# Feed-forward operands of TensorE begin at other places in a 256-byte stretch of SBUF

## The chip, the core and the metric

The kernel runs on one core of a Trainium2 chip. The time is device time in microseconds (us), from one execution to the next of the same program; the change is judged by the median of several runs. TensorE multiplies, VectorE (DVE) and ScalarE (ACT) do the elementwise work, and a DMA queue on SyncE (SP) brings the weights from HBM. SBUF has 128 partitions; where a tile "begins" below means its byte address in a partition, and only its rest after division by 256 is named.

## What is computed

Two layers, each of which holds two half-step feed-forward blocks; they are what the change touches:

```python
def swiglu(h, w1, w3, w2):
    return (jax.nn.silu(h @ w1) * (h @ w3)) @ w2
...
for l in range(DEPTH):                                   # DEPTH = 2
    x = x + 0.5 * swiglu(rms_norm(x, ffn1_norm_g[l]), ffn1_w1[l], ffn1_w3[l], ffn1_w2[l])
    ...                                                  # mixer: one projection, three branches, w_out
    x = x + cross_attention(rms_norm(x, xattn_norm_g[l]), ...)
    x = x + 0.5 * swiglu(rms_norm(x, ffn2_norm_g[l]), ffn2_w1[l], ffn2_w3[l], ffn2_w2[l])
return rms_norm(x, final_norm_g)
```

There are 256 tokens, a width of 1024 and a feed-forward width of 2816, all in float32.

## The kernel before

**Products in two parts.** TensorE works in fp32r, which keeps fewer bits of a float32. So each factor is split into a high part (the value rounded to fp32r) and a low part (what is left), and a product a·b is made as hi·hi + hi·lo + lo·hi. Weights come from HBM as float32 into `w_raw`; `_split` (L108) lets ACT write the high part `w_hi` (L126) and DVE the low part `w_lo` (L127). The activations are kept in two parts side by side: `xn` (the normed input, 8 blocks of 128 features), `g` (the inner activation, 22 blocks), `mix`, `mem_n`, `o`.

**The feed-forward products.** `ffn` (L472) goes over two column blocks of w1 and w3 at a time with `gemm_w` (L365), and at its end over w2. Each step is `mm_w` (L259), two passes of TensorE, in which a block of 128x128 weights is stationary and the activations move past it:

- the hi pass: stationary `w_hi`, moving both parts of `xn` or `g`, 512 columns;
- the lo pass: stationary `w_lo`, moving the high part alone, 256 columns.

So a stretch of feed-forward work is hi, lo, hi, lo, and so on, each with new weights. I call one hi pass and one lo pass a pair. w1 and w3 take 352 pairs in each of four blocks, w2 takes 176 in each of the first three. The last w2 is computed the other way round (`final`, L519): there the weights move, 512 columns in every pass, and `g` is stationary.

**Where tiles begin.** The tiles for `w_hi` and `w_lo` have 64 elements more than the weights need, and the weights begin `at_` elements into them (L114 to L117, table `W_AT`, L39). `xn` and `g` lie in the same manner in tiles with room to spare (`placed`, L289, with `XN_AT`, L37, and `G_AT`, L41). In the built program the tiles themselves begin 128 (`w_hi`, `w_lo`), 64 (`xn`) and 160 (`g`) past a multiple of 256, in every buffer, and a step from one block to the next is a multiple of 512 bytes. With the offset (4 bytes an element) that gives, for the passes that stand in this document, the table below; "distance" is the beginning of the stationary operand less that of the moving one.

| passes | columns | moving begins | stationary begins | distance |
|---|---|---|---|---|
| feed-forward, hi | 512 | 96 | 192 | 96 |
| feed-forward, lo | 256 | 96 | 192 | 96 |
| last w2 (weights move) | 512 | 64 | 64 | 0 |
| mixer, weights move (`w_hi<-xn` groups) | 512 | 96 | 96 | 0 |
| w_out, o, q projections | 256 | 160, 160, 96 | 128, 128, 64 | -32 |
| memory keys / values | 256 / 512 | 64 / 64 | 32 / 64 | -32 / 0 |
| attention scores and values | 256 | 160 | 160 | 0 |

**What sets the order.** A scheduler fixes the order on each engine when the program is built; it doesn't look at addresses. Weights are loaded into two buffers and split into three, so ACT and DVE work ahead of TensorE.

Of the kernel before, what the change touches and what calls it, by code (L numbers as in the profile page):

```python
# [9 lines left out]
F32R = mybir.dt.float32r  # L10
# [5 lines left out]
P = 128  # L16
# [8 lines left out]
CW = 256  # L25
# [5 lines left out]
PART_BUFS = 3  # L31
# [2 lines left out]
QE_BUFS = 1  # L34
T3_BUFS = 8
PAD = {"xn": 16, "g": 128, "mix": 0}
XN_AT = {"ffn1": 8, "mix": 8, "xattn": 8, "ffn2": 8}  # L37

W_AT = {("w13", False): 16, ("w1", False): 16, ("w3", False): 16, ("w2", False): 16, ("w2", True): 48,  # L39
        ("in", True): 56, ("kv", False): 40, ("kv", True): 48, ("out", False): 0, ("o", False): 0, "other": 48}  # L40
G_AT = (48, 40)  # L41
MIX_AT = 0
X_LOADS = ((0, 1), (1, 1), (2, 2), (4, 2), (6, 2))
T4_BUFS = 6
# [17 lines left out]
class Weights:  # L62
# [45 lines left out]
    def _split(self):  # L108
        nc, i = self.nc, self.n_split
        self.n_split += 1  # L110
        u, unit, at, nk = self.steps[i]
        while self.n_load < len(self.pieces) and self.pieces[self.n_load][0] <= u:
            self._load()
        at_ = W_AT.get((unit.key, unit.beside), W_AT["other"])  # L114
        hi = self.pool.tile([P, 4 * CW + 64], F32R, name="w_hi", tag="w_hi", bufs=PART_BUFS)[:, at_:at_ + 4 * CW]
        lo = self.pool.tile([P, 4 * CW + 64], F32R, name="w_lo", tag="w_lo", bufs=PART_BUFS)[:, at_:at_ + 4 * CW]
        if unit.key == "w13":  # L117
            hi, lo = (t[:, 0:2 * nk * CW].rearrange("p (h k c) -> p h k c", h=2, k=nk) for t in (hi, lo))
            t = self._both(u, at).rearrange("p (h k c) -> p h k c", h=2, k=nk)
        elif unit.beside:  # L120
            hi, lo = (t.rearrange("p (h k c) -> p h k c", h=2, k=2)[:, :, 0:nk, :] for t in (hi, lo))
            t = self.raw[u].rearrange("p h (k c) -> p h k c", k=4)[:, :, at:at + nk, :]
        else:
            hi, lo = (t.rearrange("p (k c) -> p k c", k=4)[:, 0:nk, :] for t in (hi, lo))
            t = self.raw[u].rearrange("p h (k c) -> p h k c", k=4)[:, at, 0:nk, :]
        self.last = nc.scalar.copy(hi, t)  # L126
        nc.vector.tensor_tensor(out=lo, in0=t, in1=hi.bitcast(F32), op=ALU.subtract)  # L127
        self.parts[i] = (hi, lo)
# [88 lines left out]
def trunk(ctx: ExitStack, tc: tile.TileContext, a: dict, out: bass.AP, stop=None, dbg=None):  # L217
# [71 lines left out]
    def placed(pool, name, k, at, **kw):  # L289

        n = k * 2 * S
        return pool.tile([P, n + PAD[name]], F32R, name=name, bufs=1, **kw)[:, at:at + n].rearrange(
            "p (k u s) -> p k u s", k=k, u=2)
# [132 lines left out]
    class Norm:  # L426


        def __init__(self, l, name, mem=False):
            self.gains = col(l, name)  # L430
            if not mem:
                self.x = placed(keep, "xn", KD, XN_AT[name.split("_")[0]], tag="xn")
            self.ssq = small.tile([P, S], F32, name="ssq", tag="ssq", bufs=2)
# [38 lines left out]
    def ffn(l, f, nrm, nxt, last=False, setup=None):  # L472
        with tc.tile_pool(name="ffn", bufs=2) as fp:
            g = placed(fp, "g", KF, G_AT[last])
            if setup is not None:
# [814 lines left out]
```

## Time and profile before

| | |
|---|---|
| median of 3 runs | 1233.04 us (1232.77 to 1233.06) |
| the profiled execution | 1232.75 us |
| its span, first to last instruction | 1231.0 us |
| TensorE (PE) busy | 1220.6 us, 99% of the span |
| weight loads (PEld) | 1100.8 us, 89% |
| DVE busy | 935.7 us, 76% |
| ACT busy | 738.3 us, 60% |
| granted TensorE clock | 0.998 of full speed |

Matmuls overlap: the next one begins before the one ahead has come out of the array, so the length of a single record (some 390 ns for 512 columns) is more than the time from one start to the next (some 230 ns). Where I speak of the time per pass, it is from start to start over a long run of passes; where I speak of the length of a record, it is compared with the length of other records of the same shape only. The numbers of the trace are rounded to 0.01 us for starts and to 1 ns for mean lengths.

### The profile page before, as it was taken

The page shows a single profiled execution, that of the slowest core. Times are in us where ns is not written, and L with a number is a line of the kernel's source. Part 1 is how long each engine was busy: PE and PEld are TensorE (multiplying, and loading weights), DVE is VectorE, ACT ScalarE, POOL GpSimd, SP SyncE. Part 2 cuts the span into 40 slices and gives each one's busy share as a digit, 9 for nine tenths or more (in the row PEclk, how much of TensorE's full clock was granted, in tenths as well). Part 3 has the DMA queues.
Part 4 walks back from the last instruction along what each step waited for, and adds up shares of the span by engine and source line. Part 5 has one row for each costly group of instructions (what it writes and reads, how often), then busy time and mean ns, then how long its engine had stood idle before and what let it go on. Part 6 is the DMA issues. An engine that isn't in the chain of part 4 may idle for free.

```text
span 1231.0 us, 21670 instructions
## 1 busy us (share of the span) xinstructions
PE 1220.6 (99%) x8378; PEld 1100.8 (89%) x8378; DVE 935.7 (76%) x1649; ACT 738.3 (60%) x1309; POOL 30.5 (2%) x54
## 2 busy tenths in 40 slices
PE   9999999999999999999999999999999999999997
PEld 8888889988999988888888888899898999888886
DVE  6989866888777687786678886679787767778754
ACT  6766645556765665664466654465677646656643
POOL 1000000000100000000000000000000000000000
PEclk9999999999999999999999999999999999999999
DMA  7645555443344345455555455544434534555453
GB/s 253 251 182 190 173 190 200 146 163 138 137 173 171 125 184 200 177 205 188 189 216 204 177 200 188 188 171 155 155 138 146 196 137 155 192 185 200 177 188 120
DMA packets 62568, 219.32 MB, mean 178 GB/s; under 512 B 6912, under 2 KB 8192, under 8 KB 62208
## 3 DMA queue, kind: packets, MB, share of 16 engines
q1 hardware_dynamic: 60976, 213.35, 47.6%
q0 software_dynamic: 768, 3.86, 0.8%
q8 instruction: 66, 1.08, 0.3%
q10 hardware_dynamic: 720, 0.72, 0.2%
q14 instruction: 38, 0.31, 0.1%
HBM read 216.85 MB, written 1.05 MB: 177 GB/s over the span
## 4 chain that ended last, share of the span: by engine, by line
PE 95%; DVE 3%; ACT 1%; issue 1%; DMA 0%; POOLq 0%; POOL 0%; ACTq 0%; DVEq 0%
PE mm L243 87%; PE aux L243 2%; PE aux L833 1%; DVE w_lo L127 1%; DVE qe L814 0%; PE aux L831 0%; DMA xT<-in_x_t_dram 0%; PE mm L241 0%; ACT w_hi L126 0%; PE aux L241 0%; DVE xc L908 0%; PE aux L826 0%; PE aux L983 0%; PE aux L912 0%; PE aux L1104 0%
## 5 line engine op out<-in xcount | busy, mean ns | idle before, releaser
L127 DVE TENSOR_TENSOR w_lo<-w_raw,w_hi 128x1024 fp32r<-128x1024 f32 (+1 forms) x411 | 494.6, 1205 | 213.5 <-ACT w_hi L126 208.3
L126 ACT CAST w_hi<-w_raw 128x1024 fp32r<-128x1024 f32 (+1 forms) x411 | 425.1, 1035 | 360.5 <-PE mm L243 217.6
L243 PE MATMUL mm<-xn,w_hi 128*128 128x512 f32 (+1 forms) x2028 | 601.1, 359 | 1.6 <-ACT ssq L440 0.9
L243 PE MATMUL mm<-xn,w_lo 128*128 128x256 f32 x1728 | 476.9, 281 | 0.0
L243 PEld LDWEIGHTS mm<-xn,w_hi 128*128 128x128 f32 x2028 | 357.6, 188 | 57.2 <-ACT w_hi L126 1.1
L243 PEld LDWEIGHTS mm<-xn,w_lo 128*128 128x128 f32 x1728 | 324.7, 188 | 3.7
L243 PE MATMUL mm<-g,w_hi 128*128 128x512 f32 x528 | 180.8, 392 | 0.0
L243 PE MATMUL mm<-g,w_lo 128*128 128x256 f32 x528 | 141.9, 280 | 0.0
L243 PEld LDWEIGHTS mm<-g,w_hi 128*128 128x128 f32 x528 | 96.6, 188 | 19.0
L243 PEld LDWEIGHTS mm<-g,w_lo 128*128 128x128 f32 x528 | 99.4, 188 | 2.9
L243 PE MATMUL mm<-w_hi,xn 128*128 128x512 f32 (+1 forms) x318 | 89.1, 374 | 0.0
L493 ACT COPY f_p<-mm 128x256 f32<-128x256 f32 x176 | 63.8, 365 | 24.5 <-PE mm L243 23.6
L494 DVE TENSOR_TENSOR f_t<-mm,f_p 128x256 f32<-128x256 f32 x176 | 73.1, 418 | 2.5 <-ACT f_p L493 2.4
L243 PEld LDWEIGHTS mm<-w_hi,xn 128*128 128x128 f32 x318 | 57.2, 188 | 9.2
L498 DVE TENSOR_TENSOR f_t<-f_t,R 128x512 f32<-128x512 f32 x88 | 60.2, 688 | 1.6 <-ACT R L462 0.4
L243 PE MATMUL mm<-w_lo,xn 128*128 128x512 f32 (+1 forms) x160 | 56.6, 378 | 1.0 <-DVE w_lo L127 1.0
L243 PE MATMUL mm<-w_hi,g 128*128 128x512 f32 x176 | 51.9, 390 | 0.0
L243 PE MATMUL mm<-mem_n,w_hi 128*128 128x256 f32 x248 | 46.7, 284 | 0.0
L243 PE MATMUL mm<-o,w_hi 128*128 128x256 f32 x248 | 46.2, 281 | 0.0
L466 DVE SCALAR_TENSOR_TENSOR xT<-mm,xT 128x256 f32<-128x256 f32 x80 | 32.1, 420 | 17.3 <-PE mm L243 17.3
L243 PE MATMUL mm<-mix,w_hi 128*128 128x256 f32 x256 | 44.8, 279 | 0.0
L243 PE MATMUL mm<-w_hi,mem_n 128*128 128x512 f32 x128 | 39.5, 393 | 0.0
(253 smaller groups left out, 1476.6 us busy)
## 6 DMA issues: line engine op xcount, KB each, us to landing
w_raw<-in_weights_dram SPq DMA_DIRECT2D x395, 512.0 KB, 4.0
w_raw<-in_weights_dram SPq DMA_DIRECT2D x18, 256.0 KB, 3.6
m_t<-in_mem_t_dram POOLq DMA_DIRECT2D x2, 1024.0 KB, 6.4
xT<-in_x_t_dram SPq DMA_DIRECT2D x3, 256.0 KB, 6.4
cst<-in_c_cst_dram POOLq DMA_DIRECT2D x1, 696.0 KB, 4.4
out_dram<-yg SPq DMA_DIRECT2D x2, 320.0 KB, 2.5
gw<-in_gates_w_dram POOLq DMA_DIRECT2D x2, 256.0 KB, 6.8
fg<-in_final_norm_g_dram POOLq DMA_DIRECT2D x1, 512.0 KB, 5.8
```

Source lines behind the costliest of these rows:

```text
L126: self.last = nc.scalar.copy(hi, t)
L127: nc.vector.tensor_tensor(out=lo, in0=t, in1=hi.bitcast(F32), op=ALU.subtract)
L243: i = self.last = nc.tensor.matmul(acc, lhsT, rhs, start=begin, stop=stop, skip_group_check=True)
L466: nc.vector.scalar_tensor_tensor(out=xT[:, j, :], in0=h, scalar=scale, in1=xT[:, j, :], op0=ALU.mult, op1=ALU.add)
L493: nc.scalar.copy(p, banks[m][:, 1, :])
L494: nc.vector.tensor_tensor(out=t[m][:, u, :], in0=banks[m][:, 0, :], in1=p, op=ALU.add)
L498: nc.vector.tensor_tensor(out=t[m], in0=t[m], in1=nrm.R[:, None, :].to_broadcast([P, 2, S]), op=ALU.mult)
L833: nc.tensor.matmul(sb[bs, i, :], ke[:, 1 + i, cb], qe[:, 1 + i, cb], start=True, stop=True, skip_group_check=True)
```

## The change

The feed-forward parts get offsets of their own, the high and the low part each its own, and `xn` (in the four feed-forward blocks) and `g` move too. All other entries keep their value, now written as a pair.

```diff
-XN_AT = {"ffn1": 8, "mix": 8, "xattn": 8, "ffn2": 8}
+XN_AT = {"ffn1": 0, "mix": 8, "xattn": 8, "ffn2": 0}
-W_AT = {("w13", False): 16, ("w1", False): 16, ("w3", False): 16, ("w2", False): 16, ("w2", True): 48,
-        ("in", True): 56, ("kv", False): 40, ("kv", True): 48, ("out", False): 0, ("o", False): 0, "other": 48}
-G_AT = (48, 40)
+W_FF = (48, 40)
+W_AT = {("w13", False): W_FF, ("w1", False): W_FF, ("w3", False): W_FF, ("w2", False): W_FF, ("w2", True): (48, 48),
+        ("in", True): (56, 56), ("kv", False): (40, 40), ("kv", True): (48, 48), ("out", False): (0, 0),
+        ("o", False): (0, 0), "other": (48, 48)}
+G_AT = (40, 40)
...
-        hi = self.pool.tile([P, 4 * CW + 64], F32R, name="w_hi", tag="w_hi", bufs=PART_BUFS)[:, at_:at_ + 4 * CW]
-        lo = self.pool.tile([P, 4 * CW + 64], F32R, name="w_lo", tag="w_lo", bufs=PART_BUFS)[:, at_:at_ + 4 * CW]
+        hi = self.pool.tile([P, 4 * CW + 64], F32R, name="w_hi", tag="w_hi", bufs=PART_BUFS)[:, at_[0]:at_[0] + 4 * CW]
+        lo = self.pool.tile([P, 4 * CW + 64], F32R, name="w_lo", tag="w_lo", bufs=PART_BUFS)[:, at_[1]:at_[1] + 4 * CW]
```

The tiles stay where they were; only the beginnings inside them move. In the built program the instructions of every engine, their order and their waits are the same as before. The feed-forward rows of the table become:

| passes | columns | moving begins | stationary begins | distance |
|---|---|---|---|---|
| feed-forward, hi | 512 | 64 | 64 | 0 |
| feed-forward, lo | 256 | 64 | 32 | -32 |

All other rows stay as they were, the last w2 among them.

## Rows read from the trace of the kernel before

**Rows 1.** The page: busy time by engine, and the chain that ended last.

```profile
PE 1220.6 (99%) x8378; PEld 1100.8 (89%) x8378; DVE 935.7 (76%) x1649; ACT 738.3 (60%) x1309; POOL 30.5 (2%) x54
PE 95%; DVE 3%; ACT 1%; issue 1%; DMA 0%; POOLq 0%; POOL 0%; ACTq 0%; DVEq 0%
```

**Rows 2.** Waits of PE: total us, times, longest.

```profile
PE mm L243 <- DVE w_lo L127: 1.0, 2, 0.5
PE mm L243 <- ACT ssq L440: 0.9, 1, 0.9
```

**Rows 3.** Feed-forward stretches: length, busy us (count) by engine, clock, DMA.

```profile
core 0: us, PE busy (x) PEld busy (x) DVE busy (x) ACT busy (x) POOL busy (x), PEclk, DMA share, GB/s
432.73:555.74 123.01, 123.01 (x713) 108.30 (x712) 99.65 (x162) 73.94 (x134) 0.70 (x1) 1.00 0.51 189
555.74:616.82 61.08, 61.08 (x354) 53.77 (x353) 37.27 (x55) 29.58 (x41) 0.00 (x0) 1.00 0.54 190
```

**Rows 4.** PE groups by shape, whole span: count, busy us, mean ns, idle before.

```profile
L243 PE MATMUL mm<-xn,w_hi 128*128 128x512 f32 x1408 | 486.9, 393 | 1.6 <-ACT ssq L440 0.9 <-DVE xn L361 0.7
L243 PE MATMUL mm<-g,w_hi 128*128 128x512 f32 x528 | 180.8, 392 | 0.0
```

**Rows 5.** The chain in order of time: start us, length us, instructions.

```profile
351.73 24.04 PE mm L243 x205
451.05 175.54 PE mm L243 x1012
1169.74 50.58 PE mm L243 x223
```

**Rows 6.** PE groups by shape, 500 to 508 us (feed-forward).

```profile
L243 PE MATMUL mm<-xn,w_hi 128*128 128x512 f32 x24 | 8.4, 392 | 0.0
L243 PE MATMUL mm<-xn,w_lo 128*128 128x256 f32 x24 | 6.7, 280 | 0.0
```

**Rows 7.** PE groups by shape, 1170 to 1220 us (last w2).

```profile
L243 PE MATMUL mm<-w_hi,g 128*128 128x512 f32 x148 | 43.1, 389 | 0.0
L243 PE MATMUL mm<-w_lo,g 128*128 128x512 f32 x74 | 26.4, 389 | 0.0
```

**Rows 8.** Timeline of PE in w_out: start us, length of the merged piece, passes.

```profile
354.13 0.28 PE L243 MATMUL mm<-mix,w_lo 128*128 128x256 f32 x1
354.25 0.39 PE L243 MATMUL mm<-mix,w_hi 128*128 128x256 f32 x2
...
355.53 0.28 PE L243 MATMUL mm<-mix,w_lo 128*128 128x256 f32 x1
```

**Rows 9.** PE groups by shape, 352 to 358 us (w_out).

```profile
L243 PE MATMUL mm<-mix,w_hi 128*128 128x256 f32 x37 | 6.5, 279 | 0.0
```

**Rows 10.** Timeline of PE in the attention scores, then their group, 402 to 403 us.

```profile
401.93 0.76 PE L243 MATMUL aux<-k_mem,att 128*128 128x256 f32 x5
402.53 0.28 PE L241 MATMUL aux<-k_mem,att 128*128 128x256 f32 x1
...
L243 PE MATMUL aux<-k_mem,att 128*128 128x256 f32 x8 | 1.2, 283 | 0.0
```

**Rows 11.** Instructions of line 243, 835.2 to 835.5 us: ns, first and last start.

```profile
L243 PE MATMUL mm<-w_lo,xn x1: 396/396/396, 835.2 to 835.2; 128*128 128x512 f32 x1
L243 PEld LDWEIGHTS mm<-xn,w_lo x1: 188/188/188, 835.2 to 835.2; 128*128 128x128 f32 x1
```

**Rows 12.** PE groups by shape, 326.51 to 326.61 us (keys to values).

```profile
L243 PE MATMUL mm<-mem_n,w_lo 128*128 128x256 f32 x1 | 0.3, 274 | 0.0
```

**Rows 13.** DVE and ACT splits by shape: 352 to 372 us, then 560 to 610 us.

```profile
L127 DVE TENSOR_TENSOR w_lo<-w_raw,w_hi 128x1024 fp32r<-128x1024 f32 x7 | 8.6, 1224 | 3.6 <-ACT w_hi L126 2.6 <-PE mm L243 0.9
L126 ACT CAST w_hi<-w_raw 128x1024 fp32r<-128x1024 f32 x8 | 8.4, 1050 | 5.5 <-PE mm L243 4.7 <-ACT sq L443 0.5
...
L127 DVE TENSOR_TENSOR w_lo<-w_raw,w_hi 128x1024 fp32r<-128x1024 f32 x17 | 20.8, 1222 | 11.6 <-ACT w_hi L126 11.5
L126 ACT CAST w_hi<-w_raw 128x1024 fp32r<-128x1024 f32 x16 | 16.8, 1049 | 18.6 <-PE mm L243 15.6 <-ACT sq L443 1.3 <-issue 1.1
```

## Prediction

> **What bounds the kernel now.** I read the page first: TensorE is busy for 99% of the span, and of the chain that ended last it holds 95% [rows 1]. Then its waits: the longest groups are 1.0 and 0.9 us, so it waits for other engines for hardly anything [rows 2]. No buffer, queue or split sets the time, then; the time of a pass on TensorE does. Third, the stretches of feed-forward work: the clock is 1.00, which is the 2.4 GHz level, DMA is at 0.51 to 0.54, and DVE, the busiest of the others, has 99.65 of 123.01 us in the w1/w3 stretch (81%) and 37.27 of 61.08 (61%) in the w2 stretch [rows 3]. Fourth, how long a pass takes from start to start, by what stands still and what moves.
>
> The change reaches 1408 + 528 = 1936 hi passes [rows 4], and a lo pass goes with each: 1936 pairs. In the chain one unbroken feed-forward piece has 1012 passes in 175.54 us, that is 506 pairs at 346.9 ns [rows 5]. So the pairs take 1936 x 346.9 ns = 672 us of the span, a little over half. One ns a pair is 1.94 us. About 0.2%, 2.5 us, is what a measurement of this kernel can tell from no change; that is 1.3 ns a pair.
>
> **What the change does, part by part.** Nothing is added, removed or put in another order on any engine, and no wait is new. Three things could still answer to a place in SBUF: the splits that write the parts, the DMAs, and TensorE's two reads.
>
> *Splits.* DVE's `w_lo` takes 1224 ns where the parts begin at 128 and 1222 ns where they begin at 192; ACT's `w_hi` takes 1050 and 1049 ns [rows 13]. I cost them at nothing: 2 ns of some 1222, and they run under TensorE's work. If TensorE gets 1% faster, DVE's share in the w1/w3 stretch goes from 81% to 82%, still no bound. The writers of `xn` and `g` are in the same case. *DMAs* write `w_raw`, which doesn't move: nothing.
>
> *TensorE's reads* are the whole of it. A pass reads its moving operand, and the load of the next stationary operand begins with it (the 512-column pass and the load for the next one both start at 835.2 us) [rows 11]. So two streams of addresses run side by side, and the question is what their distance costs. The trace has no hi pass at distance 0 followed by a lo pass at -32. It does have long runs in which all passes are alike:
>
> - 512 columns at distance 0, the last w2: 223 passes in 50.58 us, 226.8 ns each [rows 5].
> - 256 columns at -32, w_out: 12 passes lie between the starts 354.13 and 355.53 us, so 116.7 ns each [rows 8]. A longer piece, which takes in w_out and the q projection at the same distance, has 205 passes in 24.04 us, 117.3 ns [rows 5].
>
> Put together, a pair would take 226.8 + 116.7 = 343.5 ns where it takes 346.9 now: 3.4 ns less. With 117.3 it is 344.1, 2.8 ns less. The lengths of the records say the same in sign: 512 columns take 389 ns at distance 0 [rows 7] against 392 in the feed-forward stretch, 256 columns take 279 at -32 [rows 9] against 280 [rows 6]. I take 343.5, since those 12 passes are of one kind, and keep 344.1 as the nearer end.
>
> The sum: 1936 x 3.4 ns = 6.6 us. The profiled execution took 1232.75 us (span 1231.0, 1.75 us around it) and would take 1226.2; the median lies 0.3 us above the profiled one, so **1226.5 us**. With 2.8 ns it is 5.4 us and 1227.6.
>
> **Rivals.**
>
> *The load for the next pass is what counts: slower.* The sum above pairs each pass with its own stationary operand. But the operand that is read while a hi pass moves is that of the lo pass after it, at -32, and while a lo pass moves it is that of the next hi pass, at 0. In runs of like passes the two readings can't be told apart; where a run changes over they can. At 835.2 us a 512-column pass runs while weights at -32 are loaded: its record is 396 ns long, where the feed-forward hi pass has 392 and distance 0 has 389 [rows 6, 7, 11]. That speaks against my sum, by 4 ns for each hi pass. For 256 columns with the next operand at 0 there are two rows far apart: 274 ns at a single change-over [rows 12], and 283 ns in a run of attention scores, where 0.60 us for five passes (401.93 to 402.53 us) is 120 ns from start to start [rows 10]. Half way is 278.5, 1.5 under the 280 of now. So a pair gets 4 - 1.5 = 2.5 ns longer, 1936 x 2.5 = 4.8 us: 1237.9. Its ends are 4 - 6 = -2 ns (1229.2) and 4 + 3 = +7 ns (1246.6). It decides as soon as the hi pass loses more than the lo pass gains. I set it behind my sum because it rests on single passes at a change-over, while 389 against 392 and 279 against 280 are long steady runs.
>
> *Nothing happens.* The step from 343.5 to 346.9 ns may come from the mixture of 512 and 256 columns, not from the distance: no run of the trace mixes them at another distance than 96. Then the pair stays at 346.9 and the time at 1233.0. The scores speak for it too: at distance 0 a 256-column pass takes 120 ns, and 226.8 + 120 = 346.8, the pair of now. The Trainium skill points the same way (page "SBUF — State Buffer", section "Who interferes with whom"): TensorE has two read ports, one for the moving operand and one for weight loads, independent of each other, and only the pair of ports that DVE and GpSimd share causes contention. By that rule no distance matters. The trace agrees with it only in part: 283 and 279 ns for the same shape at 0 and -32 [rows 9, 10] is a difference that the rule doesn't have.
>
> *It gains more.* If the lo pass keeps the 274 ns of the change-over, 5 under the steady 279, while the hi pass has its 389, a pair takes 343.5 - 5 = 338.5 ns, and the time falls by 1936 x 8.4 = 16.3 us to 1216.8. One pass of 274 ns stands for it, and 283 against it.
>
> **How the numbers follow.** I give my forecast 46%, more gain 7%, nothing 17%, the slower rival with its upper end 30%. That makes faster by over 0.2% 53%, within 0.2% 17%, slower by over 0.2% 30%. The forecast's own range is 1223 to 1229. The range for 8 in 10 has to take in no change and the middle of the slower rival, and leaves out most of the larger gain and the upper end of the slower one: 1221 to 1241.
>
> **What would show it.** If I am right, the unbroken feed-forward piece of the chain has pairs of 343 to 344 ns, the w2 stretch of 61.08 us takes 60.5, hi records go from 392 to 389 and lo records from 280 to 279, and the last w2, w_out and the splits stay as they are. If the slower rival holds, hi records go up to some 396. If nothing happens, pairs stay at 346.9 though the records may shift between hi and lo. My forecast is wrong if the cost hangs on the operand being loaded and not on the one being used, or if it hangs on alternation itself; it is also wrong if stretches without feed-forward work move, since no address there changes.

## The result, and the profile after

The changed kernel is slower.

| | before | after |
|---|---|---|
| median | 1232.88 us (1232.39 to 1233.06, 6 runs) | 1242.71 us (1242.44 to 1243.21, 6 runs) |
| ratio, 95% interval | 1 | 1.0081 (1.0071 to 1.0092) |
| span of the profiled execution | 1231.0 us | 1241.4 us |

The forecast was 1226.5 us, the range 1221 to 1241; the time lies 1.7 us above the range. 9.8 us over 1936 pairs are 5.1 ns a pair. From here on, line numbers are two higher (L243 is now L245).

The page of the changed kernel, busy time and the chain by engine, to be held against [rows 1]:

```profile
PE 1231.4 (99%) x8378; PEld 1104.2 (89%) x8378; DVE 936.3 (75%) x1649; ACT 738.2 (59%) x1309; POOL 30.4 (2%) x54
...
PE 95%; DVE 3%; ACT 1%; issue 1%; DMA 0%; SPq 0%; POOLq 0%; POOL 0%; DVEq 0%; ACTq 0%
```

The span grew by 10.4 us and PE's busy time by 10.8 us (1220.6 to 1231.4), at the same number of instructions. Nor has a wait come up; the longest waits of PE after the change (total us, times, longest):

```profile
PE mm L245 <- DVE xn L363: 1.0, 1, 1.0
...
PE mm L245 <- DVE w_lo L129: 1.0, 2, 0.5
```

Where it went, the chain of the changed kernel tells (start us, length us, instructions), to be held against [rows 5]:

```profile
354.50 24.05 PE mm L245 x205
...
453.99 178.35 PE mm L245 x1012
...
1180.20 50.58 PE mm L245 x223
```

The same pieces, instruction for instruction: the feed-forward piece of 1012 passes grew from 175.54 to 178.35 us, or from 346.9 to 352.5 ns a pair. w_out with the q projection (24.05 us) and the last w2 (50.58 us) did not change. The starts tell how the span's 10.4 us are spread. The w_out piece begins 2.77 us later than before (354.50 less 351.73), and of feed-forward work only the first block lies ahead of it. From there to the feed-forward piece, w_out, the attention and the first 18 us of the second block together lost 0.17 us. The piece itself lost 2.81 us, the rest up to the last w2 4.71 us, and what comes after it nothing. Only stretches with feed-forward work got longer.

Within these, the records by shape from 500 to 508 us of the changed kernel (count, busy us, mean ns), to be held against [rows 6]:

```profile
L245 PE MATMUL mm<-xn,w_hi 128*128 128x512 f32 x24 | 8.5, 395 | 0.0
L245 PE MATMUL mm<-xn,w_lo 128*128 128x256 f32 x23 | 6.5, 281 | 0.0
```

The hi record went from 392 to 395 ns, where the forecast wanted 389; the lo record from 280 to 281, where it wanted 279. A timeline of PE in the same stretch (start us, length us) shows that these passes don't settle into one rhythm:

```profile
502.62 0.39 PE L245 MATMUL mm<-xn,w_hi 128*128 128x512 f32 x1
502.85 0.28 PE L245 MATMUL mm<-xn,w_lo 128*128 128x256 f32 x1
502.97 0.40 PE L245 MATMUL mm<-xn,w_hi 128*128 128x512 f32 x1
503.20 0.28 PE L245 MATMUL mm<-xn,w_lo 128*128 128x256 f32 x1
503.32 0.39 PE L245 MATMUL mm<-xn,w_hi 128*128 128x512 f32 x1
503.56 0.28 PE L245 MATMUL mm<-xn,w_lo 128*128 128x256 f32 x1
503.67 0.40 PE L245 MATMUL mm<-xn,w_hi 128*128 128x512 f32 x1
503.91 0.28 PE L245 MATMUL mm<-xn,w_lo 128*128 128x256 f32 x1
504.03 0.39 PE L245 MATMUL mm<-xn,w_hi 128*128 128x512 f32 x1
```

Hi records of 0.39 and 0.40 us take turns, and four pairs take 504.03 less 502.62, 1.41 us: 352.5 ns each. From a hi pass to the lo pass behind it are 0.23 or 0.24 us, from there to the next hi pass 0.11 or 0.12. The trace keeps starts in ns; averaged from 455 to 610 us (over some 430 pairs, without the few places where two hi or two lo passes stand side by side), a hi pass takes 232.9 ns up to the start of its lo pass, where it took 229.4 before, and a lo pass 119.9, where it took 117.4. Below, "average" means these two numbers.

The splits stayed as they were; from 565 to 615 us of the changed kernel, against [rows 13]:

```profile
L129 DVE TENSOR_TENSOR w_lo<-w_raw,w_hi 128x1024 fp32r<-128x1024 f32 x17 | 20.8, 1221 | 12.0 <-ACT w_hi L128 11.8
L128 ACT CAST w_hi<-w_raw 128x1024 fp32r<-128x1024 f32 x16 | 16.8, 1049 | 19.2 <-PE mm L245 16.0 <-ACT sq L445 1.4 <-issue 1.2
```

### The profile page after: what moved, and what is told of

Its sections match the earlier page's. It is cut to its first block, busy times and chain, and to the rows that moved or that the text cites. A ratio compares the mean times of both kernels' runs of the same rounds, so it can differ in the third digit from the quotient of the medians.

```text
span 1241.4 us, 21670 instructions
## 1 busy us (share of the span) xinstructions
PE 1231.4 (99%) x8378; PEld 1104.2 (89%) x8378; DVE 936.3 (75%) x1649; ACT 738.2 (59%) x1309; POOL 30.4 (2%) x54
## 4 chain that ended last, share of the span: by engine, by line
PE 95%; DVE 3%; ACT 1%; issue 1%; DMA 0%; SPq 0%; POOLq 0%; POOL 0%; DVEq 0%; ACTq 0%
PE mm L245 87%; PE aux L245 2%; PE aux L835 1%; DVE w_lo L129 0%; DMA xT<-in_x_t_dram 0%; DVE qe L816 0%; PE aux L833 0%; PE mm L243 0%; ACT w_hi L128 0%; PE aux L243 0%; DVE xc L910 0%; PE aux L828 0%; PE aux L985 0%; PE aux L914 0%; PE aux L1106 0%
## 5 line engine op out<-in xcount | busy, mean ns | idle before, releaser
L128 ACT CAST w_hi<-w_raw 128x1024 fp32r<-128x1024 f32 (+1 forms) x411 | 424.8, 1034 | 369.8 <-PE mm L245 226.8
L245 PE MATMUL mm<-xn,w_hi 128*128 128x512 f32 (+1 forms) x2028 | 608.8, 361 | 1.3 <-DVE xn L363 1.0
L245 PE MATMUL mm<-xn,w_lo 128*128 128x256 f32 x1728 | 478.9, 282 | 0.0
L245 PEld LDWEIGHTS mm<-xn,w_hi 128*128 128x128 f32 x2028 | 357.9, 188 | 62.3 <-DVE xn L363 1.3
L245 PEld LDWEIGHTS mm<-xn,w_lo 128*128 128x128 f32 x1728 | 324.1, 188 | 3.9
L245 PE MATMUL mm<-g,w_hi 128*128 128x512 f32 x528 | 183.2, 395 | 0.0
L245 PE MATMUL mm<-g,w_lo 128*128 128x256 f32 x528 | 142.4, 281 | 0.0
L245 PEld LDWEIGHTS mm<-g,w_hi 128*128 128x128 f32 x528 | 96.8, 188 | 20.4
L245 PEld LDWEIGHTS mm<-g,w_lo 128*128 128x128 f32 x528 | 99.2, 188 | 3.2
L245 PE MATMUL mm<-w_hi,xn 128*128 128x512 f32 (+1 forms) x318 | 89.1, 374 | 0.0
L245 PEld LDWEIGHTS mm<-w_hi,xn 128*128 128x128 f32 x318 | 57.2, 188 | 9.2
L245 PE MATMUL mm<-w_lo,xn 128*128 128x512 f32 (+1 forms) x160 | 56.6, 378 | 1.0 <-DVE w_lo L129 1.0
L245 PE MATMUL mm<-w_hi,g 128*128 128x512 f32 x176 | 51.9, 390 | 0.0
L245 PE MATMUL mm<-mem_n,w_hi 128*128 128x256 f32 x248 | 46.6, 284 | 0.0
L245 PE MATMUL mm<-o,w_hi 128*128 128x256 f32 x248 | 46.2, 281 | 0.0
L245 PE MATMUL mm<-mix,w_hi 128*128 128x256 f32 x256 | 44.8, 279 | 0.0
L245 PE MATMUL mm<-w_hi,mem_n 128*128 128x512 f32 x128 | 39.5, 393 | 0.0
```

Of the source, the lines that this page charges most:

```text
L245: i = self.last = nc.tensor.matmul(acc, lhsT, rhs, start=begin, stop=stop, skip_group_check=True)
```

## Experiments

All kernels are the changed one with other offsets, and in three of the sections with another lo pass; the diffs are against it. They are sorted by question and not by time, so an expectation can quote a kernel that stands further down. "hi 0, lo -32" gives the distances, the beginning of the stationary operand less that of the moving one, as in the tables above; only the rest by 256 counts, so 128 is -128 too. In `W_FF` (hi, lo), an offset of 48 is distance 0, 40 is -32, 32 is -64, 8 is 96 (before the change: 96 and 96) and 16 is 128.

Two readings were to be told apart first. **By use**: a pass pays for the distance of the operand that it uses; this is the sum of the forecast. **By load**: it pays for the distance of the operand that is loaded while it moves, that of the next pass; this is the slower rival.

### Which half of the change costs

```diff
-W_FF = (48, 40)
+W_FF = (48, 8)
```

> The hi half of the change alone: hi at 0, lo at 96 as before the change. If the two parts pay separately, hi 96 to 0 costs the 5.5 us that it costs with lo at 0 (1241.0 less 1235.5), so 1238.4, and the lo half has the remaining 4.3 us. If hi at 0 has its price whatever the lo part's distance, 1241 to 1243. If the loss needs both halves together, 1233.

```diff
-W_FF = (48, 40)
+W_FF = (8, 40)
```

> The lo half of the change alone: hi at 96 as before the change, lo at -32. If the two parts pay separately, the remaining 4.3 us: 1237.2. If hi at 0 has the whole price, 1233, or a few us less or more as lo at -32 stands to lo at 96. If the loss needs both halves together, 1233.

Measured: the hi half alone 1240.79 us, ratio to the kernel before 1.0066 (1.0048 to 1.0084), 8.0 us more; the lo half alone 1237.30 us, 1.0037 (1.0024 to 1.0050), 4.5 us more. The hi half comes nearest to "its price whatever the lo part's distance", the lo half to "the two parts pay separately"; no one reading gives both. Each half costs by itself, the hi part more, and together they cost 9.8 us rather than 12.6. The unbroken piece of the hi half, then of the lo half, 351.8 and 349.5 ns a pair:

```profile
452.87 177.99 PE mm L245 x1012
```

```profile
452.14 176.84 PE mm L245 x1012
```

In which pass the loss stands, the averages tell:

| hi, lo | hi pass, ns | lo pass, ns |
|---|---|---|
| 96, 96 (before) | 229.4 | 117.4 |
| 0, 96 | 234.2 | 117.6 |
| 96, -32 | 232.7 | 116.9 |
| 0, -32 (the change) | 232.9 | 119.9 |

The hi part in one line: distance 0, which in the last w2 goes with the shortest pass of 512 columns [rows 5, 7], makes the feed-forward hi pass longer. The lo part, too, makes the hi pass longer when it alone moves, and not the lo pass that uses it. Its records from 500 to 508 us say the same, against 392 and 280 before [rows 6]:

```profile
L245 PE MATMUL mm<-xn,w_hi 128*128 128x512 f32 x24 | 8.4, 395 | 0.0
L245 PE MATMUL mm<-xn,w_lo 128*128 128x256 f32 x24 | 6.7, 280 | 0.0
```

The hi pass is the one during which the lo weights are loaded (a load begins with the pass before its own, as in [rows 11]). For the lo part alone this is what the reading by load says, and not what the reading by use says. It isn't the whole: with the hi part at 0 as well, the step of the lo part from 96 to -32 lengthens the lo pass (117.6 to 119.9) and shortens the hi pass a little.

### Place or distance

```diff
-XN_AT = {"ffn1": 0, "mix": 8, "xattn": 8, "ffn2": 0}
+XN_AT = {"ffn1": 8, "mix": 8, "xattn": 8, "ffn2": 8}
-W_FF = (48, 40)
+W_FF = (56, 48)
-G_AT = (40, 40)
+G_AT = (48, 40)
```

> xn and g of the feed-forward blocks go back to 96 and both parts move with them by 32 bytes, so the distances stay 0 (hi) and -32 (lo). Load theory and unequal theory: distances alone count, so as slow as the changed kernel, 1242.7 us. Place theory: 1233 us or less.

All four operands of the feed-forward passes begin 32 bytes later; the distances remain 0 and -32. Measured: 1242.83 us, ratio 1.0081 (1.0066 to 1.0096), and the unbroken piece of the chain is the same to the last digit:

```profile
453.16 178.35 PE mm L245 x1012
```

At these two sets of places, the place by itself costs nothing. What counts is the distance between operands. This was run at distances 0 and -32 alone; the kernel with both parts at 96 and `xn` and `g` at 64, against which the halves should be held, was not run.

### Other distances: exchanged, both 0, both -32

```diff
-W_FF = (48, 40)
+W_FF = (40, 48)
```

> The two distances change places: hi parts at -32, lo parts at 0 from the moving operand, all else as in the changed kernel. Load theory (what counts is the operand that is being loaded while a pass moves): the hi pass has a load at 0, 226.8 ns, the lo pass a load at -32, 116.7 ns, so 343.5 ns a pair, 1936 pairs, 1226.5 us. Unequal theory (two different distances in one stream cost, whichever way round): as slow as the changed kernel, about 1242.7 us. Place theory (xn and g at 64 instead of 96 is what costs): also about 1242.7 us.

```diff
-W_FF = (48, 40)
+W_FF = (48, 48)
```

> Both parts at distance 0. Load theory: hi pass 226.8 ns, lo pass with a load at 0 some 120 ns as in the attention scores, 346.8 ns a pair, about 1232.7 us, the time of before. Unequal theory: the distances are equal, so no slower than before, 1233 us or less. Place theory: about 1242.7 us.

```diff
-W_FF = (48, 40)
+W_FF = (40, 40)
```

> Both parts at distance -32. Load theory: the hi pass keeps its load at -32 and with it the record of some 396 ns, about 233 ns from start to start, the lo pass has 116.7, so some 350 ns a pair, 1239 us. Unequal theory: equal distances, 1233 us or less. Place theory: about 1242.7 us.

| hi, lo | us | ratio to before (95%) |
|---|---|---|
| -32, 0 | 1229.73 | 0.9975 (0.9966 to 0.9984) |
| 0, 0 | 1241.02 | 1.0068 (1.0053 to 1.0083) |
| -32, -32 | 1233.83 | 1.0009 (0.9999 to 1.0018) |
| 0, -32 (the change) | 1242.71 | 1.0081 (1.0071 to 1.0092) |

The exchange is faster than both kernels; its piece of the chain is 345.0 ns a pair:

```profile
450.45 174.55 PE mm L245 x1012
```

Taking the hi part from 0 to -32 saves 8.9 us with the lo part at -32, and 11.3 us with the lo part at 0. Taking the lo part from -32 to 0 saves 4.1 us with the hi part at -32, and 1.7 us with the hi part at 0. In both the shorter pass of the runs of like passes (0 for 512 columns, -32 for 256) is the dearer one here. That falsifies the sum by use with those prices. By load, the sign of both is right, but not the sizes and the order: it gave 1226.5, 1232.7 and 1239 us for the three kernels, and both parts at 0 came out slower than both at -32. The other two ideas of the expectations fall as well: unlike distances as such (the exchange has them and is fast, both at 0 has none and is slow), and the place of `xn` and `g` (the exchange has the new place). With both parts at 0, the loss stands in the hi pass itself, as the timeline of that kernel shows:

```profile
502.84 0.40 PE L245 MATMUL mm<-xn,w_hi 128*128 128x512 f32 x1
503.08 0.28 PE L245 MATMUL mm<-xn,w_lo 128*128 128x256 f32 x1
503.19 0.40 PE L245 MATMUL mm<-xn,w_hi 128*128 128x512 f32 x1
503.43 0.28 PE L245 MATMUL mm<-xn,w_lo 128*128 128x256 f32 x1
503.54 0.40 PE L245 MATMUL mm<-xn,w_hi 128*128 128x512 f32 x1
503.78 0.28 PE L245 MATMUL mm<-xn,w_lo 128*128 128x256 f32 x1
503.90 0.40 PE L245 MATMUL mm<-xn,w_hi 128*128 128x512 f32 x1
504.14 0.28 PE L245 MATMUL mm<-xn,w_lo 128*128 128x256 f32 x1
```

From every hi pass to its lo pass are 0.24 us, from every lo pass to the next hi pass 0.11 or 0.12; the averages are 235.7 and 116.6 ns. With the hi part at -32, the lo part's distance again moves the hi pass alone: the averages are 226.7 and 118.1 ns with lo at 0, 229.2 and 118.2 with lo at -32. In the last w2 the same shape at the same distance 0 takes 226.8 ns.

### Used or loaded

To part the two readings, the lo pass moves other columns: the stationary operands stay, and the moving operand of the lo pass alone begins elsewhere. The lo product is then not that of the reference.

```diff
-            self.mm(self.ap[:, 1, :], wl, x[:, 0, :], False, stop)
+            self.mm(self.ap[:, 1, :], wl, x.rearrange("p u s -> p (u s)")[:, 8:8 + S], False, stop)
```

> The changed kernel, but the lo pass moves 256 columns that begin 32 bytes further on (8 columns; it multiplies the wrong columns, so the low part of each feed-forward product is not the reference's; counts and sizes stay). Stationary operands stay at 64 (hi) and 32 (lo), the hi pass still moves from 64. So hi weights are loaded at -32 from what moves meanwhile (the lo pass), but are still used at 0 from their own moving operand. Load theory (the distance to the pass during which weights are loaded counts): like both parts at -32, about 1233.8 us. Use theory (the distance to the pass that uses them counts): as slow as the changed kernel, 1242.7 us.

The hi weights are used at 0 and loaded while operands move whose beginning is 32 bytes behind theirs. Measured: 1241.83 us, ratio 1.0072 (1.0055 to 1.0088), and in the chain 352.0 ns a pair, against 352.5 for the change and 347.5 for both at -32. Its piece, then that of both at -32:

```profile
452.78 178.12 PE mm L245 x1012
```

```profile
451.21 175.86 PE mm L245 x1012
```

The hi pass keeps its loss (235.6 ns on the average) though its weights are now loaded at -32 from what the lo pass moves. That speaks against the reading by load for the hi weights. That the price goes with the operand that the hi pass uses would fit, but is not shown: the edit also took the lo pass's own distance from -32 to -64, whose price no run gives alone.

```diff
-W_FF = (48, 40)
+W_FF = (40, 48)
...
-            self.mm(self.ap[:, 1, :], wl, x[:, 0, :], False, stop)
+            self.mm(self.ap[:, 1, :], wl, x.rearrange("p u s -> p (u s)")[:, 56:56 + S], False, stop)
```

> The exchanged offsets (hi 32, lo 64), but the lo pass moves 256 columns that begin at 32 (56 columns further on; again the wrong columns are multiplied in the low part). Hi weights are now loaded at 0 from what moves meanwhile and used at -32; lo weights are loaded at 0. Load theory: like both parts at 0, about 1241.0 us. Use theory: as fast as the exchanged offsets, 1229.7 us.

Here the hi weights are used at -32 and loaded at 0. Measured: 1235.98 us, ratio 1.0024 (1.0015 to 1.0034): between the two readings and equal to neither. It doesn't decide. The lo pass's own distance went from 0 to 32 with the edit, and this may be what costs; no run has it alone.

### All passes of 512 columns

If the exchange of signs comes from the short lo pass, it has to vanish where the lo pass moves as many columns as the hi pass. These kernels multiply `w_lo` by both parts of the activation, one product more than the reference has.

```diff
-W_FF = (48, 40)
+W_FF = (48, 48)
...
-            self.mm(self.ap[:, 1, :], wl, x[:, 0, :], False, stop)
+            self.mm(self.ap, wl, x, False, stop)
```

> Both parts at distance 0, and the lo pass moves all 512 columns too (it adds the product of the two low parts; nothing is left out). Room theory (a load at 0 costs only where it has hardly more time than it needs, in the 256-column pass): every pass like the last w2, 226.8 ns, so 1936 pairs at 453.6 instead of 346.9 ns, 1233 + 206.6 = 1439 us, and not slower than the same kernel at -32. Distance theory (0 costs more than -32 in any pass): slower than the same kernel at -32 by about the 7 us that stand between both at 0 and both at -32 now.

The second has the same edit of the lo pass and `W_FF = (40, 40)`:

> Both parts at distance -32, and the lo pass moves all 512 columns. Room theory: 226.8 to 230 ns a pass, 1439 to 1452 us, as slow as the same kernel at 0 or slower. Distance theory: about 7 us faster than the same kernel at 0.

The third and fourth have `(40, 48)` and `(48, 40)`:

> Lo passes move 512 columns (so lo times low activation is added to the result); hi at -32, lo at 0. With 512 columns everywhere, both parts at 0 gave 1438.25 us and both at -32 gave 1463.55. If the pass length alone turns the sign and each part pays for its own distance, hi at -32 costs half of the 25.3 us: about 1450.9. If the lo part's distance does all of it, 1438.3; if the hi part's distance does all of it, 1463.5. If being unlike costs by itself, more than 1463.5.

> Lo passes move 512 columns; hi at 0, lo at -32. Each part pays for its own: about 1450.9. All with the lo part: 1463.5. All with the hi part: 1438.3. If being unlike costs by itself, more than 1463.5.

| hi, lo, both of 512 columns | us | ns a pair in the chain |
|---|---|---|
| 0, 0 | 1438.25 | 453.4 |
| -32, -32 | 1463.55 | 466.7 |
| -32, 0 | 1463.20 | 466.4 |
| 0, -32 | 1463.30 | 466.4 |

The unbroken piece of the chain of the first kernel, then of the third:

```profile
508.30 229.18 PE mm L245 x1011
```

```profile
515.51 235.78 PE mm L245 x1011
```

With 512 columns in every pass, both parts at 0 take 226.7 ns a pass, the 226.8 of the last w2 [rows 5]: the row that the forecast took is true of such streams. The sign is the other way round than with the short lo pass: with the lo part at 0, the hi part is better at 0 than at -32 here, and worse there. And the price is no sum over operands: one part at -32 costs the whole 25 us, and the second one nothing more. Each of the last two kernels fits one of its outcomes (all with the hi part for the third, all with the lo part for the fourth), but no outcome fits both. The records of the fourth (hi 0, lo -32) from 520 to 680 us show why, where those of the first are all 389 ns:

```profile
L245 PE MATMUL mm<-xn,w_hi 128*128 128x512 f32 x300 | 118.6, 396 | 0.0
L245 PE MATMUL mm<-xn,w_lo 128*128 128x512 f32 x301 | 118.4, 394 | 0.0
```

Both passes get longer: the hi pass, during which the lo weights at -32 are loaded, to 235.0 ns from start to start (averaged over this stretch), and the lo pass, which uses them, to 231.7. In the third kernel it is the other way round, 231.7 for the hi pass and 235.0 for the lo pass, during which the hi weights at -32 are loaded. So here the operand that is loaded and the one that is used both have a price, and the first is the larger. The 396 ns are those of the change-over that the slower rival started from [rows 11].

### A lo pass of 384 columns

A further idea: behind a short lo pass the load of the hi weights runs on into the hi pass, and reads there at the same rest as the moving operand. A lo pass of 384 columns leaves the load half as much room again. These two kernels move half of the low part too in the lo pass.

```diff
-W_FF = (48, 40)
+W_FF = (48, 48)
...
-            self.mm(self.ap[:, 1, :], wl, x[:, 0, :], False, stop)
+            self.mm(self.ap.rearrange("p u s -> p (u s)")[:, 2 * S - 384:], wl, x.rearrange("p u s -> p (u s)")[:, 0:384], False, stop)
```

> Both parts at distance 0, the lo pass moves 384 columns instead of 256 (which columns it adds to the low part is not the reference's). Tail theory (a weight load takes about as long as a pass of 256 columns, runs on into the next pass and collides there with the first reads of that pass's own moving operand; that is why hi at 0 costs after a short lo pass and not after one of 512 columns): with 384 columns the load is done in time, some 227 + 173 = 400 ns a pair, 1336 us, and not slower than the same kernel with hi at -32. Use theory (the distance of hi to its own moving operand costs by itself): slower than the kernel with hi at -32 by the 11.3 us that stand between e2 and e1.

The other one has `W_FF = (40, 48)`:

> The same with hi at -32, lo at 0, 384 columns in the lo pass. Tail theory: as fast as the kernel before it in this list, or slower by a few us, because a load at -32 costs under a pass longer than 256 columns (1336 to 1345 us). Use theory: 11.3 us faster than it.

Measured: 1358.43 us at hi 0, 1347.77 us at hi -32, lo at 0 in both. Their pieces of the chain, first 413.4, then 406.6 ns a pair:

```profile
484.86 210.19 PE mm L245 x1017
```

```profile
483.26 206.75 PE mm L245 x1017
```

Hi at 0 costs 10.7 us with 384 columns, nearly the 11.3 us that it costs with 256. So the idea falls with the load's length that the expectation gave it, about that of a pass of 256 columns. It doesn't fall altogether: the record of a load is 188 ns long [rows 11], and in the first of these two kernels the lo pass takes 176.0 ns on the average, from 520 to 680 us. There a load of hi weights and the hi pass that uses them:

```profile
520.06 0.19 PEld L245 LDWEIGHTS mm<-xn,w_hi 128*128 128x128 f32 x1
```

```profile
520.23 0.40 PE L245 MATMUL mm<-xn,w_hi 128*128 128x512 f32 x1
```

By these records the load still ends inside the hi pass with 384 columns, as with 256, and no longer with 512, where a pass takes 226.7 ns. That is where the sign changes. Whether the record is the true length of a load, and whether the overlap is the cause, no run shows; a lo pass of 448 columns would be a test. The change of sign comes somewhere between 384 and 512 columns, or with the two passes being of one length.

### Further distances

256 columns in the lo pass again, only `W_FF` is changed: (8, 48), (16, 48), (40, 16), (32, 48).

> hi at distance 96 as before the change, lo at 0, 256 columns in the lo pass, result unchanged. Tail theory: hi at 96 was as good as at -32 before (346.9 ns a pair with lo at 96 too), and lo at 0 under the 512-column pass is the best known, so 1228 to 1231 us. Use theory: the same. If hi and lo have to stand at one distance to each other, 1233 us or more.

> hi at distance 128, lo at 0, result unchanged. A place that no run has had. Tail theory says no more than that the load's end must not meet the first reads of the hi pass, and half a 256-byte stretch away is the farthest there is: 1226 to 1231 us. If the places repeat every 128 bytes, 128 is the same as 0: 1241 us.

> 256-column lo passes again; hi at -32, lo at +128. If places repeat every 128 bytes for the lo part as they nearly did for the hi part (hi at 128: 1241.9, hi at 0: 1241.0), this takes the 1229.7 us of hi -32, lo 0. If only the rest by 256 counts, it takes something else: 1233.8 (lo at -32) is the nearest known.

> 256-column lo passes; hi at -64, lo at 0. Known for lo 0: hi 0 gives 1241.0, hi -32 gives 1229.7, hi 96 gives 1235.5, hi 128 gives 1241.9. If only hi at 0 (or 128) is bad and any other distance is good, 1229.7 to 1235.5. If -32 is a narrow good place between bad ones, about 1241. If it gets better the farther the weights begin ahead of the activations, below 1229.7.

| hi, lo | us | ratio to before (95%) |
|---|---|---|
| 128, 0 | 1241.92 | 1.0074 (1.0062 to 1.0087) |
| 0, 0 | 1241.02 | 1.0068 (1.0053 to 1.0083) |
| 96, 0 | 1235.52 | 1.0022 (1.0013 to 1.0031) |
| -32, 128 | 1234.93 | 1.0017 (1.0008 to 1.0027) |
| -32, 0 | 1229.73 | 0.9975 (0.9966 to 0.9984) |
| -64, 0 | 1222.83 | 0.9918 (0.9904 to 0.9933) |

With lo at 0, the hi part alone moves the time over 19 us. Distances 0 and 128 are the worst and 0.9 us apart; 96 and -32, which also differ by 128, are 5.8 us apart; so 128 bytes are nearly a period for the hi part, and not quite. For the lo part they are none: 0 and 128 differ by 5.2 us. By its distance from the nearest multiple of 128, the hi part takes 1241.0 and 1241.9 us at 0 bytes, 1229.7 and 1235.5 at 32, 1222.8 at 64: the farther, the faster, in the five places that were run. Hi at 96 missed the 1228 to 1231 us that both theories gave and lies in the third outcome (1233 or more), hi at 128 took the 1241 of a period of 128 bytes, and hi at -64 the outcome "the farther". Hi -64, lo 0 is 10.0 us faster than the kernel before and 19.9 us faster than the change. Its page, its piece of the chain and a timeline of PE:

```profile
PE 1211.1 (99%) x8378; PEld 1094.9 (90%) x8378; DVE 935.2 (77%) x1649; ACT 738.1 (60%) x1309; POOL 30.5 (2%) x54
```

```profile
449.64 172.52 PE mm L245 x1012
```

```profile
502.73 0.39 PE L245 MATMUL mm<-xn,w_hi 128*128 128x512 f32 x1
502.96 0.28 PE L245 MATMUL mm<-xn,w_lo 128*128 128x256 f32 x1
503.07 0.39 PE L245 MATMUL mm<-xn,w_hi 128*128 128x512 f32 x1
503.30 0.28 PE L245 MATMUL mm<-xn,w_lo 128*128 128x256 f32 x1
503.41 0.39 PE L245 MATMUL mm<-xn,w_hi 128*128 128x512 f32 x1
503.64 0.28 PE L245 MATMUL mm<-xn,w_lo 128*128 128x256 f32 x1
503.75 0.39 PE L245 MATMUL mm<-xn,w_hi 128*128 128x512 f32 x1
503.98 0.28 PE L245 MATMUL mm<-xn,w_lo 128*128 128x256 f32 x1
504.09 0.39 PE L245 MATMUL mm<-xn,w_hi 128*128 128x512 f32 x1
```

Every hi record has 0.39 us now, from hi to lo are 0.23 and from lo to hi 0.11 us each time. Four pairs take 1.36 us, 340 ns each; over the whole piece it is 340.9 ns, and the averages are 227.2 and 113.6 ns. That is less than the 343.5 of the forecast: behind a hi pass at -64, a 256-column pass at 0 costs less than the 120 ns that it takes in a run of like passes [rows 10], and less than w_out's 116.7 [rows 8].

## Why the prediction was wrong

**What bounds the kernel: right.** TensorE's passes set the time, no other engine came into the way at 10 us more or 10 us less, and all of the difference lies in feed-forward stretches. The unbroken piece stands a little above the average of all pairs: it lost 5.6 ns a pair, where the 10.4 us of the same execution are 5.4 ns a pair.

**Splits and DMAs at nothing: right.** 1221 and 1049 ns after, 1222 and 1049 before [rows 13], no new wait.

**Distance, not place: right**, as far as the kernel with everything 32 bytes later shows it.

**226.8 + 116.7: the step that failed.** I took the price of a pass at a distance from runs in which all passes are alike, and added two such prices. The first of them is true where it was read: all passes of 512 columns with both parts at 0 take 226.7 ns each. It does not carry over to a stream in which 512 columns take turns with 256. There the hi part at 0 costs 5.4 to 8.0 us against 96, 8.9 to 11.3 us against -32 and 18.2 us against -64. The pair came to 352.5 ns, 9 above the sum: the hi pass took 232.9 ns on the average instead of 226.8, the lo pass 119.9 instead of 116.7. The second price was wrong in the same way: the lo half of the change, from 96 to -32, cost 4.5 us where it was to save some. It cost them in the hi pass, so the step that gave each pass the price of its own stationary operand failed too; the prediction had read that the load of the next weights begins with a pass [rows 11], and left it out of the sum. The prediction named the first part itself, as "it hangs on alternation itself", but gave the mixture no price of its own beyond leaving the pair at 346.9.

**The records as a second witness: not one.** The 389 and the 279 came from the same runs of like passes as the starts, so they repeated the same assumption. In the feed-forward stretch the hi record went to 395 ns, not to 389, and the lo record to 281, not to 279.

**The slower rival: right in sign, half right in mechanism.** Its change-over at 835.2 us (396 ns with the next weights at -32) [rows 11] foretold the hi record: 395 ns after the change, 395 with the lo part alone at -32, 396 in the 512-column kernel with the same distances. I had set it behind the steady rows because it was a single pass. Its lo pass did not come true: it was to gain 1.5 ns and lost 2.5 on the average, and the other change-over, 274 ns [rows 12], was no guide. Nor had it a price for the hi part at 0, which alone made the hi pass 4.8 ns longer; and with the hi weights loaded at -32 and used at 0 that loss remained (1241.83 us). So its 1237.9 fell 4.8 us short. I cut the range at 1241, under the rival's upper end of 1246.6, and the time fell into the part that was cut.

**Nothing happens: wrong.** This rival, and the rule beside it from the Trainium skill ("SBUF — State Buffer", section "Who interferes with whom"), have no price for distance. The runs measure 20 us between hi -64, lo 0 and the change, at the same instructions in the same order. Here the measurement decides.

**What stays open.** Why a hi pass takes longer at 0 than at -32 when the pass ahead of it moves 256 or 384 columns, and shorter when it moves 512, with the lo part at 0 each time. A price by the operand in use, in runs of like passes, fails on the exchange of the offsets and on the lo part alone; a price by the operand being loaded fits the lo part with the hi part at 96 or -32, and fails for the hi part, on the lo pass moved by 32 bytes; a price that adds over the operands fails on the four kernels with 512 columns. The load of the hi weights running on into the hi pass fits where the sign changes if a load takes the 188 ns of its record, but no run tests it. The finding is thus a table of times by distance, not a mechanism. Neither -64 for the lo part alone nor -64 in the 512-column kernels was run.

## What to carry to other kernels

Where TensorE is busy throughout, the beginnings of its two operands against each other are worth a few runs: here they moved the time from 1222.8 to 1242.7 us with no instruction changed. Try them in the very stream that is to get faster, hi and lo offsets together: of the offsets tried, the best one of a run of like passes was among the worst in a stream of long and short passes. Where a forecast adds prices from uniform stretches, none of its rows shows the mixture; a single row at a change-over can point the right way (396 ns here) or the wrong way (274 ns), so keep the range wide until the mixture itself has run.

## What the runs showed of the hardware

- TensorE's pace with a new weight block in every pass depends on the rest of the operands' distance: 340.9 to 352.5 ns for a pass of 512 columns with one of 256, at a granted clock of 1.00 (the 2.4 GHz level) and the same instructions.
- Lo weights at distance -32 instead of 96, with the hi weights at 96 in both, lengthen the hi pass that runs while they are loaded (229.4 to 232.7 ns), and not the lo pass that uses them (117.4 and 116.9 ns).
- With 512 columns in each pass there are only two levels among four kernels, 226.7 ns a pass with both parts at 0 and 233.2 or 233.4 with one or both at -32.
- For the hi part distances 0 and 128 cost the same within 0.9 us; for the lo part they do not (5.2 us).
- An offset of 32 bytes on all four operands of the feed-forward passes together costs nothing (1242.83 against 1242.71 us).
